# First pair of the second FFN as plain block products inside the pool mixer's last steps, with the pool stage in a written order

## The chip, the cores and the metric

The kernel runs on one core of a Trainium2 chip. The core has a matrix engine (TensorE, PE in the profile), a vector engine (VectorE, DVE), a scalar engine (ScalarE, ACT), a general engine (GpSimd, POOL) and an engine whose queue starts transfers (SyncE, SP); 16 DMA engines move data between HBM and the on-chip memory. Each engine works through its own instructions in their order and waits where an operand is not ready. Times are microseconds (us) of the device for one launch.

## The reference, cut to what matters

Two layers of an encoder over 512 prompt rows and 32 sample rows (544 tokens), model width 1024. Layer 0 mixes with attention and a recurrence, layer 1 with a trailing-window pooling; each mixer is followed by a SwiGLU feed-forward (FFN) of inner width 2816. All is float32.

```
def rmsnorm(x, g):   y = x * rsqrt(mean(x*x) + EPS) * g
def swiglu(x, wg, wu, wd):   return (silu(x @ wg) * (x @ wu)) @ wd

def pool_mixer(xn, buf, start_pos, pool_w, pool_scale):
    for gi, win in enumerate((2, 4, 8, 16)):          # four groups of 256 channels
        outs.append((end - begin) / cnt - xf[:, POOL_BUF:, sl])   # trailing mean minus identity
    y = einsum('btgc,gcd->btgd', stack(outs), pool_w) * pool_scale

for layer in range(2):
    x = x + mixer(rmsnorm(x, norm_mix[layer]))
    x = x + swiglu(rmsnorm(x, norm_ffn[layer]), ffn_gate[layer], ffn_up[layer], ffn_down[layer])
return rmsnorm(x, norm_final), ...states
```

## The kernel before

Activations are held channel-major: `x` is 8 blocks of 128 channels by 544 tokens, and the tokens are cut into two halves of 272. To keep float32 accuracy a product is three matmuls: each operand is split in a high part (rounded by ACT, `AF.Copy` into a reduced type) and a low part (the difference, by DVE); high*high, high*low and low*high are summed in PSUM. "Splitting" a 128x1024 weight tile is one ACT and one DVE instruction (L822, L823).

**FFN.** The 2816 inner channels are 22 blocks f, taken as 11 pairs fp. For a pair, gate and up (u = 0, 1) times the two halves of the 8 channel blocks is a 2x2 block product. It is done with seven products in place of eight (Strassen-Winograd): `strassen` makes 14 steps of 12 matmuls of 272 columns (168 in all), whose weight operands are sums such as t1, t2, t3, t4 and whose activation operands are sums that the class `Forms` builds (b11, n1, n2, b21, t3, t4, b22), once per FFN. `Forms.add(k)` is called for each channel block k as it becomes final; blocks 4 to 7 build all the mixed sums.

`Supply` holds the weights: 17 slots of 128x1024, and a list of operations (load, add, split) with due times counted in beats (`beat.tick`, one per step or per down bank). Sums of weight blocks are formed partly by a second DMA that accumulates (issued by POOL, L836) and partly by DVE (L845). `need(n)` runs the list until n is there. `rows` supplies the down weights; the last pair's rows have the due times in L785.

`down(fp)` adds the hidden blocks of earlier pairs into `x`: 8 banks of 12 or 24 matmuls per pair, in two PSUM buffers `sm`, each followed by a DVE add into `x` (L1000). They are spread over the 14 steps of the pair by L1040. For the pairs 1 and 2 only two hidden blocks are due, so that a bank there is 6 matmuls. `last_down` does the rest of the first FFN's down product (L1019, L1025) and calls `after0`, which makes the norm and splits for the pool mixer. `final` does that for the second FFN together with the output norm.

**Pool stage** (from L1147 on). For six token tiles t and two channel halves i, `pool_in` multiplies by the pool weights (12 matmuls of 256 columns), `pool_mid` evicts with the row's norm factor `rt` (by ACT or DVE in turn), `pool_out(m)` multiplies by the window bands and adds channel block m into `x` (two DVE instructions, L1210), then calls `n3.add(m)`. From m = 4 on the first steps of the second FFN's pair 0 stand between the `pool_out`s. In this stage only PE's order is written by hand (`manual_schedule(engines={PE})`); the order of DVE, ACT and SP is chosen by the compiler's scheduler. In the FFNs the order of PE, DVE, ACT and SP is as written; POOL's is chosen by the scheduler everywhere.

Of the kernel before, what the change touches and what calls it, by code (L numbers as in the profile page):

```python
# [14 lines left out]
P = 128  # L15
# [16 lines left out]
def kernel(  # L32
# [226 lines left out]
    class Forms(Norm):  # L259
# [35 lines left out]
        def add(self, k):  # L295
            j, g = k % 4, col(self.gcol + k)
            x0, x1 = x[:, k, :HN], x[:, k, HN:]
            if k < 4:
                if j % 2 == 0:
                    self.d[j], self.d[j + 1] = self.tmp(j // 2)  # L300
                d = self.d[j]
                self.put("b11", j, x0, g)
                ve.tensor_tensor(d, x0, x1, op=ALU.subtract)
                self.put("n1", j, d, g)
            else:
                d, g0 = self.d[j], col(self.gcol + j)
# [10 lines left out]
            self.square(k)  # L317

# [454 lines left out]
    class Supply:  # L773
# [94 lines left out]

        def ahead(self):
# [33 lines left out]
    ORDER = (("a11", "b11"), ("t1", "n1"), ("t2", "n2"), ("t3", "t3"), ("a12", "b21"), ("a22", "t4"), ("t4", "b22"))  # L903

    def strassen(sup, nin, fp, hid):
# [3 lines left out]
        def product(i, u):  # L909
# [43 lines left out]
            elif i == 5:  # L953
# [5 lines left out]
                hidden(2, out[:, 1], 1)  # L959
# [3 lines left out]
            elif i == 6:  # L963
                ve.tensor_tensor(out[:, 0, h1], o, pb, op=ALU.add)
                beat.later(1, lambda: ve.tensor_mul(out[:, 0], out[:, 0], s[:, 0]))  # L965
                hidden(1, out[:, 0], 0)

        def hidden(n, t, i):
            f = 2 * fp + i
            a, b = [hp.tile([P, T], F32R, tag=f"h{p}{f % 6}", name=nm("h" + p)) for p in "hl"]  # L970

            def low():
                ve.tensor_tensor(b, t, a.bitcast(F32), op=ALU.subtract)
                hid[f] = a, b

            beat.later(n, lambda: ac.activation(a, t, AF.Copy))  # L976
            beat.later(n + 1, low)
# [3 lines left out]
    def ffn(sup, nin, after=None, mid={}, last=None, first=None):  # L981
# [85 lines left out]
    def bands():  # L1067
        eye = big.tile([P, P], F32, name="eye")[:, :BW]
        gp.memset(eye, 1.0)
        band(eye, 1, 15)  # L1070
        eyl = cst.tile([P, NL], F32, name="eyl")[: NL + 15]
        gp.memset(eyl, 1.0)
        band(eyl, 1, 15)
        for g, win in enumerate(WINDOWS):
# [71 lines left out]
    with tc.manual_schedule(engines=queues):  # L1146
        ffn(supply, n1[0], after0, {(0, 3): lambda: scales(n1[0]), (0, 7): lambda: n1[0].out(), (1, 4): bands,  # L1147
# [44 lines left out]
    n3 = Forms(16 + 8, 0)  # L1192

    def pool_out(m):
# [16 lines left out]
        n3.add(m)  # L1211

    with tc.manual_schedule(engines={mybir.EngineType.PE}):
        ps = [(small(), 0), (small("z"), 0), (small("z"), 0)]
        for t in range(3):
            pool_in(ps[t][0], t, 0)
            if t == 2:
                rt = n2.rs_tok([(0, j, a2[:, c : c + n]) for j, (c, n) in enumerate(TS)] + [(0, 6, na30)])
        for t in range(3):
            pool_mid(ps[t][0], t, 0, t % 2)  # L1220
        todo = [(3, 0), (4, 0), (5, 0), (0, 1), (1, 1), (2, 1), (3, 1), (4, 1), (5, 1)]
        for j, (t, i) in enumerate(todo):
            if j % 2 == 0:
                pa = one("pa"), one("pb")
            pool_in(pa[j % 2], t, i)
            if j % 2:
                for b, (t, i) in enumerate(todo[j - 1 : j + 1]):
                    pool_mid(pa[b], t, i, b)
            if j == 5:
                supply.need(("t1", 0))  # L1230
                pool_out(0)
            if j == 7:
                pool_out(1)
        pool_mid(pa[0], 5, 1, 0)
# [3 lines left out]
        prods = strassen(supply, n3, 0, first)
        for m in range(4, KD):
            pool_out(m)  # L1240
            if m == 7:
                give(*ptm, *ptb)
            if m in (4, 6):
                pool_state(m == 6)
            prods.pop(0)()
        prods.pop(0)()
        prods.pop(0)()
        scales(n3)
        for f in prods[:2]:
            f()  # L1250
# [104 lines left out]
```

## Time and profile before

| | us |
|---|---|
| runs of the kernel (3) | 1100.87, 1104.32, 1105.19; median 1104.32 |
| profiled execution, its own time | 1103.79 |
| its span, first to last instruction | 1102.0 |
| PE busy | 1044.4 (95%) |
| DVE busy | 768.4 (70%) |
| ACT busy | 491.7 (45%) |

The span is 1.8 us shorter than the execution's own time. PE is the engine that is nearly always busy, so that what counts are the few places where it waits and those where its clock is lower; matmuls overlap, so that the distance of two starts, and not the length of one, is what a matmul costs. In a row of the timeline the bracket is the idle time ahead of it and what ended it.

### The profile page before, as it was taken

How to read it: one execution, taken by the hardware profiler on the slowest of the kernel's cores; microseconds unless marked ns; L12 is line 12 of the kernel's file. 1: busy time of each engine (PE TensorE's matmuls, PEld its weight loads, DVE VectorE, ACT ScalarE, POOL GpSimd, SP SyncE). 2: the span in 40 equal slices, each digit the busy share in tenths (PEclk: the TensorE clock that was granted, in tenths of full speed). 3: DMA queues.
4: the chain of work that ended last, by engine and by line, in shares of the span. 5: the costliest groups of instructions: out<-in, count | busy, mean ns of one | idle time of the engine just before them, and what ended most of it. 6: DMA issues, size and time to landing. Idle time of an engine off the chain costs nothing.

```text
span 1102.0 us, 19760 instructions
## 1 busy us (share of the span) xinstructions
PE 1044.4 (95%) x7971; PEld 1002.9 (91%) x7971; DVE 768.4 (70%) x1236; ACT 491.7 (45%) x825; POOL 210.7 (19%) x331
## 2 busy tenths in 40 slices
PE   8979999999899999999999989599999999999987
PEld 7978888899899999999999878499999999999976
DVE  6776666767777777767776575957777766677643
ACT  7555555544643344332444354644434434334422
POOL 5162225103421101111110211111011111010100
PEclk8989999999999999999999998889999999999999
DMA  8412222414877467756566532256655676656602
GB/s 221 140 50 68 68 58 90 106 52 106 158 158 144 106 120 168 173 135 132 125 127 153 128 88 34 62 116 148 139 116 122 146 172 149 135 122 125 167 33 81
DMA packets 210955, 130.63 MB, mean 119 GB/s; under 512 B 7224, under 2 KB 195872, under 8 KB 210865
## 3 DMA queue, kind: packets, MB, share of 16 engines
q1 hardware_dynamic: 162528, 103.11, 33.2%
q0 software_dynamic: 47696, 25.16, 17.6%
q8 instruction: 62, 1.02, 0.4%
q10 hardware_dynamic: 640, 1.12, 0.3%
q14 instruction: 29, 0.23, 0.1%
HBM read 124.76 MB, written 4.60 MB: 117 GB/s over the span
## 4 chain that ended last, share of the span: by engine, by line
PE 75%; DVE 10%; issue 6%; ACT 5%; DMA 2%; POOL 1%; SPq 0%; ACTq 0%; DVEq 0%; POOLq 0%
PE xy L925 30%; PE sm L997 17%; PE z L925 11%; PE acc L168 10%; ACT ha L822 2%; DVE la L823 2%; DVE sB L474 1%; DMA raw<-in_hyb_w_in_dram 1%; PE ps L1019 1%; PE pa L1173 1%; POOL sA L493 1%; ACT y L1294 1%; DVE y L1300 1%; DMA rt<-in_ffn_up_dram 1%; DVE lt L823 1%
## 5 line engine op out<-in xcount | busy, mean ns | idle before, releaser
L997 PE MATMUL sm<-hh,h 128*128 128x272 f32 x576 | 168.0, 292 | 7.0 <-DVE x L1000 6.2
L836 POOL DMA_DIRECT2D rt<-in_ffn_gate_dram x44 | 57.0, 1295 | 589.4 <-DMA rt<-in_ffn_gate_dram 382.3
L997 PE MATMUL sm<-hl,h 128*128 128x272 f32 x576 | 165.6, 287 | 0.0
L997 PE MATMUL sm<-hh,l 128*128 128x272 f32 x576 | 165.4, 287 | 0.0
L823 DVE TENSOR_TENSOR lt<-rt,ht 128x1024 fp32r<-128x1024 f32 x88 | 107.9, 1226 | 50.7 <-ACT ht L822 50.6
L997 PEld LDWEIGHTS sm<-hh,h 128*128 128x128 f32 x576 | 108.4, 188 | 11.3 <-DVE x L1000 11.3
L98 ACT ACTIVATE s<-s 128x544 f32<-128x544 f32 x44 | 29.0, 659 | 187.1 <-DVE s L934 182.4
L997 PEld LDWEIGHTS sm<-hh,l 128*128 128x128 f32 x576 | 108.4, 188 | 0.0
L997 PEld LDWEIGHTS sm<-hl,h 128*128 128x128 f32 x576 | 108.4, 188 | 0.0
L925 PE MATMUL xy<-b,ha 128*128 128x272 f32 x704 | 103.6, 289 | 0.8 <-DVE x L678 0.8
L823 DVE TENSOR_TENSOR la<-ra,ha 128x1024 fp32r<-128x1024 f32 x66 | 81.0, 1227 | 29.1 <-ACT ha L822 29.1
L822 ACT ACTIVATE ht<-rt 128x1024 fp32r<-128x1024 f32 x88 | 92.5, 1051 | 11.5 <-DVE rt L845 6.1
L925 PEld LDWEIGHTS xy<-b,ha 128*128 128x128 f32 x704 | 93.9, 188 | 1.3 <-DVE x L678 1.0
L1000 DVE TENSOR_TENSOR x<-x,sm 128x272 f32<-128x272 f32 x160 | 69.2, 432 | 31.8 <-PE sm L997 30.8
L168 PE MATMUL acc<-xh,whi 128*128 128x272 f32 x320 | 75.4, 317 | 2.5 <-ACT xh L98 2.5
L836 POOL DMA_DIRECT2D rt<-in_ffn_up_dram x44 | 76.5, 1739 | 2.0 <-DMA rt<-in_ffn_up_dram 1.5
L976 ACT ACTIVATE hh<-u 128x544 fp32r<-128x544 f32 x44 | 29.0, 659 | 97.5 <-DVE u L965 49.9
L822 ACT ACTIVATE ha<-ra 128x1024 fp32r<-128x1024 f32 x66 | 67.3, 1051 | 6.1 <-DMA ra<-in_ffn_up_dram 4.9
L168 PE MATMUL acc<-xl,whi 128*128 128x272 f32 x320 | 68.2, 294 | 0.5 <-DVE xl L228 0.5
L168 PE MATMUL acc<-xh,wlo 128*128 128x272 f32 x320 | 67.9, 293 | 0.0
L925 PE MATMUL xy<-n,ht 128*128 128x272 f32 x352 | 54.1, 295 | 11.4 <-DVE n L293 6.9
L943 ACT ACTIVATE c<-xy 128x272 f32<-128x272 f32 x44 | 17.5, 398 | 95.2 <-PE xy L925 95.2
(381 smaller groups left out, 2525.1 us busy)
## 6 DMA issues: line engine op xcount, KB each, us to landing
r<-in_ffn_down_dram SPq DMA_DIRECT2D x44, 512.0 KB, 6.0
ra<-in_ffn_gate_dram SPq DMA_DIRECT2D x66, 256.0 KB, 5.3
ra<-in_ffn_up_dram SPq DMA_DIRECT2D x66, 256.0 KB, 6.8
rt<-in_ffn_gate_dram SPq DMA_DIRECT2D x44, 256.0 KB, 3.3
rt<-in_ffn_up_dram SPq DMA_DIRECT2D x44, 256.0 KB, 4.5
rt<-in_ffn_gate_dram POOLq DMA_DIRECT2D x44, 256.0 KB, 6.0
rt<-in_ffn_up_dram POOLq DMA_DIRECT2D x44, 256.0 KB, 7.1
raw<-in_hyb_w_in_dram SPq DMA_DIRECT2D x20, 512.0 KB, 3.9
```

What stands on the lines that cost most here:

```text
L98: i = ac.activation(*a, **k).ins
L168: pe.matmul(ps[:, h, : s.stop - s.start], lhsT=a[:, wi, :], rhs=b[:, s], start=first and j == 0, stop=last and j == 2)
L474: ve.tensor_tensor_scan(r, r, r, 1.0, op0=ALU.mult, op1=ALU.min)
L493: gp.affine_select(t[:, N - P :], t[:, N - P :], pattern=[[-1, P]], compare_op=ALU.is_gt, fill=fill, base=0, channel_multiplier=1)
L822: ac.activation(hi, raw, AF.Copy)
L823: ve.tensor_tensor(lo, raw, hi.bitcast(F32), op=ALU.subtract)
L836: gp.dma_start(v(t)[:, u], w, accum_op=ALU.add)
L925: pe.matmul(o, lhsT=lt, rhs=r, start=first and n == 0, stop=n == 11, skip_group_check=True)
L943: ac.activation(pc, o, AF.Copy)
L976: beat.later(n, lambda: ac.activation(a, t, AF.Copy))
L997: pe.matmul(ps, lhsT=lt[:, c], rhs=r[:, s], start=i == 0 and j == 0, stop=i == len(fs) - 1 and j == 2)
L1000: ve.tensor_add(xs, xs, ps)
```

## The change

1. The second FFN's pair 0 is no longer done by `strassen` but by `plain`: 2 blocks f x 2 (gate, up) x 8 channel blocks x 2 token halves x 3 = 192 matmuls. Its weights are the four plain blocks a11, a12, a21, a22 (8 loads by SP, 4 splits), without t1, t2, t3, t4 (14 loads, 4 of them accumulating by POOL, 7 splits and 2 DVE adds).
2. `LateForms.add(k)` makes only the split of block k's two token halves; DVE's part of block k is held back until the next `pool_out`. The mixed sums for pair 1 come from `sums()`, 16 steps that are placed between the matmuls of the plain pair.
3. The pool stage has its order written for PE, DVE, ACT and SP. All six `pool_in` of the first channel half now stand ahead of the matmuls for the norm (`rs_tok`).
4. For pairs 1 and 2 of both FFNs the down banks come one per step from step 4 on, in place of three in a row behind step 5 and then one per step.
5. The last pair's down rows are due 4 to 10 beats earlier. The window bands are emitted at four places in place of one.

```
-            self.rows(PAIRS, ((-9, -5), (-8, -3), (-3, 3), (-1, 5)))
+            self.rows(PAIRS, ((-15, -9), (-14, -8), (-12, -6), (-11, -4)))
...
+        def plain(self, fp):
+            for j, (t0, t1) in enumerate(((-20, -12), (-18, -10), (-6, 2), (-2, 5))):
+                n = f"a{j // 2 + 1}{j % 2 + 1}", fp
+                self.blocks(t0, n, (2 * fp + j // 2, j % 2))
+                self.split(t1, n, n)
...
-                    for _ in range(0 if n < 5 else 3 if n == 5 else 1):
+                    few = len(sup.due(fp)[0]) < 4
+                    for _ in range(n > 3 if few else 0 if n < 5 else 3 if n == 5 else 1):
...
+    class LateForms(Forms):
+        def add(self, k):
+            g = col(self.gcol + k)
+            bs = [(x[:, k, s], *self.block(k, h)) for h, s in HALVES]
+            for src, h, _ in bs:
+                ac.activation(h, src, AF.Copy, scale=g)
+            t = self.acc if k == 0 else s2.tile([P, T + NS], F32, tag="nsq", name=nm("nsq"), bufs=1)[:, :T]
+            ac.activation(t, x[:, k], AF.Square)
+            def low():
+                for src, h, l in bs:
+                    ve.scalar_tensor_tensor(l, src, g, h.bitcast(F32), op0=ALU.mult, op1=ALU.subtract)
+                if k:
+                    ve.tensor_add(self.acc, self.acc, t)
+            return low
...
+        def mm(i, us, k, bank=None):
+            for u in us:
+                n = f"a{i + 1}{k // 4 + 1}", 0
+                wh, wl = [v(w)[:, u, k % 4] for w in sup.need(n)]
+                for h in range(2):
+                    if k == 0:
+                        acc[i, u, h] = bank()[:, :HN]
+                    bh, bl = nin.block(k, h)
+                    for j, (a, b) in enumerate(((wh, bh), (wh, bl), (wl, bh))):
+                        pe.matmul(acc[i, u, h], lhsT=a, rhs=b, start=k == 0 and j == 0, stop=k == KD - 1 and j == 2,
+                                  skip_group_check=True)
...
+        for t in range(6):
+            into(t, 0)
+        rt = n2.rs_tok([(0, j, a2[:, c : c + n]) for j, (c, n) in enumerate(TS)] + [(0, 6, na30)])
+        into(0, 1)
+        mid(*[(t, 0) for t in range(6)])
...
+        supply.need(("a12", 0))
         pool_out(3)
+        for m in range(4, KD + 4):
+            if m < KD:
+                pool_out(m)
...
+            elif low:
+                low.pop()()
+                sums = n3.sums()
+            beat.tick(supply)
+            mm(0, (0, 1), m - 4, lambda: one("f0"))
...
+        for k in range(KD):
+            mm(1, (0,), k, lambda: small("z"))
+            sums.pop(0)()
+            if k == 2:
+                scales(n3)
         n3.out()
+        for k in range(KD):
+            if k == 1:
+                gate_out(0)
+            if k == 4:
+                up_out(0)
+            mm(1, (1,), k, small)
+            if sums:
+                sums.pop(0)()
+        gate_out(1)
+        beat.later(3, lambda: up_out(1))
```

DVE in the first FFN's `last_down`, before: `x<-x,ps` adds a finished bank, `xs` and `nacc` are the pool mixer's split and norm sum; `la`, `lt` are splits and `rt` a sum of weights for the second FFN's pair 0.

```order
L1025 TENSOR_TENSOR x<-x,ps_7480 128x272
L1025 TENSOR_TENSOR x<-x,ps_7481 128x272
L823 TENSOR_TENSOR la_1119_7874<-ra_1105_7723,ha_1118_7873 128x1024
L823 TENSOR_TENSOR lt_1121_7878<-rt_1104_7718,ht_1120_7877 128x1024
L845 TENSOR_TENSOR rt_1165_8053<-rt_1104_7718,ra_1105_7723 128x1024
L228 SCALAR_TENSOR_TENSOR xs_7536<-x,cols,xs_7536 128x544
L219 TENSOR_TENSOR nacc_7494<-nacc_7494,nsq_7539 128x544
L1025 TENSOR_TENSOR x<-x,ps_7522 128x272
```

The same place in the changed kernel:

```order
L1143 TENSOR_TENSOR x<-x,ps_7480 128x272
L1143 TENSOR_TENSOR x<-x,ps_7481 128x272
L228 SCALAR_TENSOR_TENSOR xs_7536<-x,cols,xs_7536 128x544
L219 TENSOR_TENSOR nacc_7494<-nacc_7494,nsq_7539 128x544
L1143 TENSOR_TENSOR x<-x,ps_7522 128x272
```

The three weight instructions of 128x1024 have left the chain of adds.

PE in pair 1 of the second FFN, before: the first down banks (`sm`), the first two of three in a row, between step 5 (`xy_8470`) and step 6.

```order
L925 MATMUL xy_8470<-n_1147_8014,lt_1230_8448 128x272 x4
L997 MATMUL sm_8560<-hh_8398,h_1237_8486 128x272
L997 MATMUL sm_8560<-hl_8399,h_1237_8486 128x272
L997 MATMUL sm_8560<-hh_8398,l_1238_8487 128x272
L997 MATMUL sm_8560<-hh_8433,h_1237_8486 128x272
L997 MATMUL sm_8560<-hl_8434,h_1237_8486 128x272
L997 MATMUL sm_8560<-hh_8433,l_1238_8487 128x272
L997 MATMUL sm_8570<-hh_8398,h_1237_8486 128x272
L997 MATMUL sm_8570<-hl_8399,h_1237_8486 128x272
```

In the changed kernel the first bank stands behind step 4, and a step of the pair follows it:

```order
L1054 MATMUL xy_8417<-n_1190_8260,lt_1214_8421 128x272 x4
L1115 MATMUL sm_8522<-hh_8461,h_1223_8463 128x272
L1115 MATMUL sm_8522<-hl_8462,h_1223_8463 128x272
L1115 MATMUL sm_8522<-hh_8461,l_1224_8464 128x272
L1115 MATMUL sm_8522<-hh_8378,h_1223_8463 128x272
L1115 MATMUL sm_8522<-hl_8379,h_1223_8463 128x272
L1115 MATMUL sm_8522<-hh_8378,l_1224_8464 128x272
L1054 MATMUL xy_8443<-n_1190_8260,ht_1213_8420 128x272
```

Each bank is now apart from the next by a step of 12 matmuls, and the first one reads the second hidden block (`hh_8461`, `hl_8462`) one step earlier.

DVE behind the last norm sum of the pool stage, in the changed kernel: splits of weights (a22 of pair 0, a11 and t1 of pair 1), then the first of the 16 steps of `sums()`.

```order
L346 TENSOR_TENSOR nacc_7718<-nacc_7718,nsq_8137 128x544
L903 TENSOR_TENSOR la_1180_8173<-ra_1154_8029,ha_1179_8172 128x1024
L903 TENSOR_TENSOR la_1182_8177<-ra_1155_8032,ha_1181_8176 128x1024
L903 TENSOR_TENSOR lt_1184_8205<-rt_1153_8024,ht_1183_8204 128x1024
L378 TENSOR_TENSOR tmp_8154<-x 128x544
L378 TENSOR_TENSOR tmp_8155<-x 128x544
L925 TENSOR_TENSOR rt_1187_8232<-rt_1153_8024,ra_1155_8032 128x1024
L370 SCALAR_TENSOR_TENSOR n_1186_8222<-tmp_8154,cols,n_1185_8221 128x272 x2
L370 SCALAR_TENSOR_TENSOR n_1186_8222<-tmp_8155,cols,n_1185_8221 128x272 x2
L373 SCALAR_TENSOR_TENSOR tmp_8158<-tmp_8154,cols,tmp_8156 128x272 x2
L195 RECIPROCAL rt_8271<-rt_8271 128x4
```

Before, weight splits and the forms for pair 0 alternate here, and pair 0's own steps wait for them:

```order
L823 TENSOR_TENSOR lt_1199_8235<-rt_1166_8055,ht_1198_8234 128x1024
L293 SCALAR_TENSOR_TENSOR t_1154_8029<-tmp_8010,t_1153_8028 128x272
L823 TENSOR_TENSOR lt_1201_8252<-rt_1167_8060,ht_1200_8251 128x1024
L293 SCALAR_TENSOR_TENSOR n_1148_8015<-tmp_8098,n_1147_8014 128x272
L290 TENSOR_TENSOR b_1155_8032<-tmp_8144,b_1155_8032 128x272
L293 SCALAR_TENSOR_TENSOR t_1152_8024<-tmp_8099,t_1151_8023 128x272
```

What the plain pair's matmuls need is made ahead of this place; what is made here is for pair 1.

## Rows read from the trace of the kernel before

**Rows 1.** Busy time by engine in two stretches (span, PE, PEld, DVE, ACT, POOL, clock, DMA).

```profile
700.00:720.00 20.00, 9.33 (x44) 8.27 (x44) 17.42 (x31) 9.23 (x20) 2.69 (x2) 0.66 0.33 71
...
1000.00:1050.00 50.00, 49.89 (x397) 49.46 (x396) 35.37 (x53) 19.52 (x28) 5.73 (x5) 1.00 0.54 128
```

**Rows 2.** Timeline of PE, third bank of a burst (start, length, line, operation, [idle]).

```profile
308.77 0.39 PE L997 MATMUL sm<-hh,h 128*128 128x272 f32 x1 [1.54 <-DVE x L1000]
...
337.68 0.39 PE L997 MATMUL sm<-hh,h 128*128 128x272 f32 x1 [1.54 <-DVE x L1000]
...
747.00 0.39 PE L997 MATMUL sm<-hh,h 128*128 128x272 f32 x1 [1.61 <-DVE x L1000]
...
775.91 0.39 PE L997 MATMUL sm<-hh,h 128*128 128x272 f32 x1 [1.56 <-DVE x L1000]
```

**Rows 3.** Timeline of PE, last down product of the first FFN.

```profile
639.83 0.36 PE L1019 MATMUL ps<-hh,h 128*128 128x272 f32 x1 [0.78 <-DVE x L1025]
...
645.17 0.39 PE L1019 MATMUL ps<-hh,h 128*128 128x272 f32 x1 [2.10 <-DVE x L1025]
```

**Rows 4.** Timeline of DVE at that place.

```profile
639.95 1.22 DVE L823 TENSOR_TENSOR la<-ra,ha 128x1024 fp32r<-128x1024 f32 x1
641.09 1.22 DVE L823 TENSOR_TENSOR lt<-rt,ht 128x1024 fp32r<-128x1024 f32 x1
642.22 1.22 DVE L845 TENSOR_TENSOR rt<-rt,ra 128x1024 f32<-128x1024 f32 x1
```

**Rows 5.** Timeline of PE at the start of the output stage.

```profile
1065.69 0.41 PE L1285 MATMUL sm<-h,hh 128*32 128x512 f32 x1 [2.69 <-ACT h L822]
...
1066.95 0.42 PE L1285 MATMUL sm<-l,hh 128*32 128x512 f32 x1 [0.61 <-DVE l L823]
```

**Rows 6.** Timeline of PE in the pool stage.

```profile
663.19 2.33 PE L243 MATMUL sm<-ones,nacc 128*128 128x1 f32 x12 [4.48 <-DVE nacc L219]
...
671.35 0.40 PE L1173 MATMUL pb<-pwh,xs 128*128 128x256 f32 x2
...
672.78 0.40 PE L1173 MATMUL pa<-pwh,xs 128*128 128x256 f32 x2
...
675.63 0.38 PE L1207 MATMUL z<-bf,ptm 128*128 128x128 f32 x2
...
677.17 0.51 PE L1173 MATMUL pa<-pwh,xs 128*128 128x256 f32 x2
```

**Rows 7.** Timeline of PE, norm sums in the first FFN.

```profile
272.12 1.10 PE L243 MATMUL sm<-ones,nacc 128*128 128x1 f32 x10
```

**Rows 8.** Timeline of PE, pair 0 and pair 1 of the second FFN.

```profile
700.34 1.27 PE L925 MATMUL z<-n,ht 128*128 128x272 f32 x8 [1.98 <-DVE x L1210]
...
711.81 0.59 PE L925 MATMUL xy<-n,ht 128*128 128x272 f32 x1 [3.44 <-ACT n L292]
714.53 0.59 PE L925 MATMUL xy<-n,ht 128*128 128x272 f32 x1 [2.12 <-DVE n L293]
...
734.70 1.17 PE L925 MATMUL xy<-b,ha 128*128 128x272 f32 x8
...
736.21 1.17 PE L925 MATMUL xy<-b,ha 128*128 128x272 f32 x8
...
743.74 0.28 PE L997 MATMUL sm<-hh,h 128*128 128x272 f32 x1
```

**Rows 9.** Timeline of DVE in the pool stage.

```profile
693.04 0.49 DVE L1210 SCALAR_TENSOR_TENSOR x<-sm,cols,x 128x272 f32<-128x272 f32 x1
693.46 0.71 DVE L219 TENSOR_TENSOR nacc<-nacc,nsq 128x544 f32<-128x544 f32 x1
694.09 0.43 DVE L293 SCALAR_TENSOR_TENSOR n<-tmp,n 128x272 fp32r<-128x272 f32 x1
```

**Rows 10.** Timeline of ACT at the second FFN's norm factor.

```profile
720.90 1.28 ACT L92 ACT_TABLE_LOAD   x1
```

More of the change, by code (lines that the diff above doesn't have):

```diff
@@ L773, with __init__ @@
     class Supply:
-        def __init__(self, l):
+        def __init__(self, l, plain=False):
             self.l, self.raw, self.w, self.start = l, {}, {}, None
@@ L781, in __init__ @@
             for fp in range(PAIRS):
-                self.base = 22 * fp - 8 * bool(fp)
-                self.pair(fp)
+                self.base = 22 * fp - (6 if plain else 8) * bool(fp)
+                (self.pair if fp or not plain else self.plain)(fp)
             self.base += 22
-            self.rows(PAIRS, ((-9, -5), (-8, -3), (-3, 3), (-1, 5)))
+            self.rows(PAIRS, ((-15, -9), (-14, -8), (-12, -6), (-11, -4)))
             self.ops.sort(key=lambda o: o[0])
@@ L903, with hidden, low, plain @@
     ORDER = (("a11", "b11"), ("t1", "n1"), ("t2", "n2"), ("t3", "t3"), ("a12", "b21"), ("a22", "t4"), ("t4", "b22"))
+    def hidden(n, t, f, hid):
+        a, b = [hp.tile([P, T], F32R, tag=f"h{p}{f % 6}", name=nm("h" + p)) for p in "hl"]
+        def low():
+            ve.tensor_tensor(b, t, a.bitcast(F32), op=ALU.subtract)
+            hid[f] = a, b
+        beat.later(n, lambda: ac.activation(a, t, AF.Copy))
+        beat.later(n + 1, low)
+    def plain(sup, nin, hid):
+        s, out = [sc.tile([P, 2 * T], F32, tag=t, bufs=1, name=nm(t)).rearrange("p (f c) -> p f c", f=2) for t in "su"]
+        acc = {}
+        def mm(i, us, k, bank=None):
[9 more added lines that the diff above has]
+                                  skip_group_check=True)
+            if k % 4 == 3 and us[-1]:
+                sup.done(n)
+        def gate_out(i):
+            for h, c in HALVES:
+                ve.tensor_mul(s[:, i, c], acc[i, 0, h], nin.r[:, c])
+            beat.later(1, lambda: act(s[:, i], s[:, i], AF.Silu))
+            beat.later(2, lambda: ve.tensor_mul(s[:, i], s[:, i], nin.r))
+        def up_out(i):
+            for h, c in HALVES:
+                ve.tensor_mul(out[:, i, c], acc[i, 1, h], s[:, i, c])
+            hidden(1, out[:, i], i, hid)
+        return mm, gate_out, up_out
     def strassen(sup, nin, fp, hid):
@@ L958, in product @@
                 beat.later(1, up)
-                hidden(2, out[:, 1], 1)
+                hidden(2, out[:, 1], 2 * fp + 1, hid)
             elif i == 6 and u == 0:
@@ L965, in product @@
                 beat.later(1, lambda: ve.tensor_mul(out[:, 0], out[:, 0], s[:, 0]))
[L966 to L977, printed above, removed]
+                hidden(1, out[:, 0], 2 * fp, hid)
         return [lambda i=i, u=u: product(i, u) for i in range(7) for u in range(2)]
@@ L1065, in band, with bands @@
         gp.affine_select(o, o, pattern=[[-1, n]], compare_op=ALU.is_ge, fill=0.0, base=win - 1 - off, channel_multiplier=1)
[L1067 to L1074, printed above, removed]
+    eye = big.tile([P, P], F32, name="eye")[:, :BW]
+    eyl = cst.tile([P, NL], F32, name="eyl")[: NL + 15]
+    def bands(*gs):
+        if 0 in gs:
+            gp.memset(eye, 1.0)
+            band(eye, 1, 15)
+            gp.memset(eyl, 1.0)
+            band(eyl, 1, 15)
+        for g in gs:
+            win = WINDOWS[g]
             gp.memset(bf[:, g], 1.0 / win)
@@ L1190, in pool_state @@
         gp.dma_start(pl_p[0, 0][:, 512 * hf : 512 * (hf + 1)], so[15:30])
-    n3 = Forms(16 + 8, 0)
+    n3 = LateForms(16 + 8, 0)
+    low = []
     def pool_out(m):
@@ L1210, in pool_out @@
             ve.scalar_tensor_tensor(xs, pp[:, :HN], col(40 + m), xs, op0=ALU.mult, op1=ALU.add)
[L1211 to L1234, printed above, removed]
+        if low:
+            low.pop()()
@@ new lines, in pool_out, with into, mid @@
+        low.append(n3.add(m))
+    with tc.manual_schedule(engines=queues):
+        supply = Supply(1, plain=True)
+        for _ in range(2):
+            supply.ops.pop(0)[2]()
+        banks = {}
+        def into(t, i):
+            banks[t, i] = (small if t == 0 and not i else lambda: small("z") if t < 3 and not i else one("pi"))()
+            pool_in(banks[t, i], t, i)
+        def mid(*ts):
+            for n, (t, i) in enumerate(ts):
+                pool_mid(banks[t, i], t, i, n % 2)
+        for t in range(6):
[3 more added lines that the diff above has]
+        mid(*[(t, 0) for t in range(6)])
+        into(1, 1)
+        into(2, 1)
+        mid((0, 1), (1, 1))
+        pool_out(0)
+        into(3, 1)
+        mid((2, 1))
+        into(4, 1)
+        pool_out(1)
+        mid((3, 1))
+        into(5, 1)
@@ L1235 @@
         pool_out(2)
+        mid((4, 1), (5, 1))
+        supply.need(("a12", 0))
         pool_out(3)
         first = {}
[L1238 to L1250, printed above, removed]
-        n3.out()
@@ L1252 @@
-        for f in prods[2:]:
-            f()
+        mm, gate_out, up_out = plain(supply, n3, first)
+        for m in range(4, KD + 4):
+            if m < KD:
+                pool_out(m)
+                if m in (4, 6):
+                    pool_state(m == 6)
+                if m == 7:
+                    give(*ptm, *ptb)
+            elif low:
+                low.pop()()
+                sums = n3.sums()
+            beat.tick(supply)
+            mm(0, (0, 1), m - 4, lambda: one("f0"))
+            if m == KD + 3:
+                sums.pop(0)()
+                sums.pop(0)()
```

62 lines of the change are left out of this document (58 added, 4 removed).

## Prediction

> **What bounds the kernel now.** I read first the busy times by slice and the clock, then the chain of waits, then the brackets in PE's timeline, and last DVE's and ACT's timelines at the places where PE waits. The first view shows that PE has no room over most of the span: in a stretch of the second FFN it is busy for 49.9 of 50 us at full clock, with DVE at 35.4 [rows 1]. There a saving on another engine is worth nothing, and a matmul more costs its distance: twelve of 272 columns take 736.21 - 734.70 = 1.51 us, 0.126 each [rows 8]. The second view puts nearly all of the rest on DVE and ACT. The brackets tell where. Up to a few long ones in the first half that the change doesn't touch, they are four kinds:
> - behind two banks of a down burst, PE waits for DVE's add into `x`: 1.54, 1.54, 1.61, 1.56 [rows 2], in pairs 1 and 2 of each FFN, sum 6.25;
> - in the first FFN's last down product, 0.78 and 2.10 [rows 3], sum 2.88;
> - at the start of the output stage, 2.69 and 0.61 [rows 5], sum 3.30;
> - in the pool stage and the second FFN's pair 0: 4.48 ahead of the norm sums [rows 6], then five gaps of 2.0 to 3.4 between 698 and 715 [rows 8]. Here PE has 9.3 us of work in 20, DVE 17.4, and the clock is 0.66 [rows 1]: DVE is the engine that sets the pace.
>
> **The change part by part.** All is reckoned in the profiled execution, 1103.79 us (its span of 1102.0 and 1.8 around it), 0.5 under the median of the runs.
>
> *Bursts.* Three banks of six matmuls (0.75 us each) stand in a row, with two buffers; the third needs the first one's add, which stands on DVE behind a weight split. With one bank per step, 1.51 us of other matmuls come between two banks. All four brackets go: -6.25. What is late next: the first bank now comes one step earlier and reads the hidden blocks of the pair before; in three of the four cases those are split by ordinary steps with a step's time in hand. The fourth, behind the plain pair, is in the stage's sum below. If the cover is missing, each place keeps about what it had.
>
> *Last down product.* Between two adds DVE does two splits and a sum of weights for the old pair 0: 639.95 to 643.36, three at a distance of 1.14 [rows 4]; PE waits behind them. They move behind the pool stage's start, where they are counted below: -2.88.
>
> *Down rows of the last pair.* Four splits of 1.14 (4.6 on DVE) go into the last pair's steps, where DVE has 14.6 us of 50 free [rows 1]; the output stage's two brackets go, since nothing else is late there (the hidden blocks are made by the last pair's own steps): -3.30. If that cover were gone, the price would be at most the 3.30.
>
> *Bands.* They are emitted later, but POOL's own order stays as it was but for four accumulating loads that are gone: 0. POOL has 5.7 us of 50 busy in the FFN [rows 1]; were a band's work to fall ahead of an accumulating load, the load still has a dozen beats until its split.
>
> *Pool stage and pair 0.* I take it from the end of the third `pool_in` (663.19 - 4.48 = 658.7) [rows 6] to the first down bank of pair 1, 743.74 [rows 8]: 85.0 us before. For the new order I walk the three written queues, each instruction starting when its engine is free and its operands are there.
>
> PE alone: nine `pool_in` at 1.43 (672.78 - 671.35), eight `pool_out` at 1.54 (677.17 - 675.63) [rows 6], the plain pair's 192 matmuls at 0.126 (24.2; 24 more than before, 3.0), five steps of pair 1 (7.6), two sets of norm sums at full clock (about 1.4 and 1.1, by 1.10 for ten [rows 7]), some 1.5 for small transposes: 12.9 + 12.3 + 24.2 + 7.6 + 2.5 + 1.5 = 61.0. It would be there at 719.7. The three `pool_in` that now stand ahead of the norm sums fill the 4.48; one wait for a PSUM buffer of about 1.4 comes in its place, since the evictions need the norm. `pool_out(3)` ends at about 680.6.
>
> DVE from there to the split of the second hidden block, which the first bank reads: five `pool_out` updates and six low splits (22 of 272), mixed sums (16 of 272), the gates and products of the plain pair (8), so 46 at 0.42; 18 of 544 at 0.63 [rows 9]; nine of 1024 (splits of a11, a12, a21, a22, of a11, t1 and t2 of pair 1, one of down rows, and one sum) at 1.14 [rows 4]: 19.3 + 11.3 + 10.3 = 40.9, with small things 41.5, so 722 if it never waits. In the walk it waits 9.4 more: twice for ACT's half of a weight split that stands behind squares (1.7 and 2.4), 2.4 at the root of the norm, where ACT reloads its table (1.28 [rows 10]) on both sides of it, and the rest in pieces under 1.2. So the second hidden block is split at 732, and the bank starts at 732.2. PE's waits in the walk: about 2.0 ahead of `pool_out(4)`, 3.5 ahead of the norm's spread, 2.1 at step 2 of pair 1 (its `z` bank is held until DVE has read the plain pair's gate), 1.7 at the bank.
>
> Before, six steps precede the first bank, now five: one step, 1.51, is still to come. 732.2 + 1.5 = 733.7, against 743.74: -10.0. DVE saves three splits and two sums (5.7) and has half of its forms' work behind the plain matmuls; PE pays 3.0. Bounds: PE's order alone gives 719.7 + 1.5, so -22.5; DVE without a wait gives 722.5 + 1.5, so -19.7; with twice the waits 741.6 + 1.5, so -0.6. I take the walk's own value, as its durations are rows of the same instructions.
>
> Sum: -6.25 - 2.88 - 3.30 - 10.0 = -22.4; 1103.8 - 22.4 = **1081.4 us**.
>
> The clock: after the 4.48 without matmuls the norm sums are at half rate, 2.33 for twelve against 1.10 for ten [rows 6, 7], the lower of the two levels, 1.2 GHz in place of 2.4; after 1.98 the next eight matmuls take 1.27 against 1.17, so full [rows 8]. The gap of 3.5 lies between. The Trainium skill (TensorE: Matmul & The Clock Gate, "HAM oscillation — how this bites in real kernels") says that waits between bursts drop the array to half rate, so that each next burst starts slow; the rows agree for the long gap and not for the short one. By that rule the second half of the plain pair would run at half rate, 48 matmuls and 6.0 us longer; by the row of 1.98, none. As DVE is behind PE there by 3.8 (2.1 and 1.7), the sum by the rule would be 1081.4 + 2.2.
>
> **The rivals.**
> - *PE sets the pace* (DVE and ACT never late). For: 41.5 us of DVE against 39 of PE from `pool_out(3)` on. Against: the root of the norm sits in ACT's queue behind the second step of `sums()`. Time: 1081.4 - 9.7 (DVE's bound) = 1071.7, by PE's bound 1068.9.
> - *The stage gains nothing.* The order written by hand has waits in series that the walk sees too small (ACT, DVE, ACT for each form, PSUM buffers held by late evictions); twice the 9.4 does it. For: each wait is on an engine that stands still with work behind it. Against: five gaps and half rate are to be beaten. Time: 1103.8 - 12.4 + 0 to -0.6 = 1091.
> - *The bursts don't go:* the bank one step earlier waits for the hidden block as long as it did for the add. For: it is 2.3 us sooner. Against: no bracket shows PE waiting for a hidden block now. Time: 1081.4 + 6.25 = 1087.7.
> - *Slower: the clock.* PE falls to half rate at the norm gap or earlier and, with the gaps at `pool_out(4)`, step 2 and the bank, stays there. Each us of matmuls then costs one more, first against DVE's lead. From `pool_out(4)` to the first bank PE has 39 us of work; all of it at half rate ends at 680.6 + 78 = 758.6, so 26.4 later than forecast, 1107.8. It decides from about 35 us of full-rate work done slowly (22.4 and the 12.5 by which DVE is later than PE). For: the stretch from 700 to 720 at 0.66 now [rows 1]. Against: full rate after 1.98.
>
> **How the numbers follow.** Forecast 0.60 (own range 1076 to 1087), PE sets the pace 0.16, stage gains nothing 0.14, bursts stay 0.06, slower by the clock 0.04. The range for 8 in 10 runs from near the first rival's time to the second's: 1071 to 1092. A measurement of this kernel can tell about 0.5% (5.5 us) from no change. All cases but the last lie below 1098.8: faster 0.94; the last one's smaller forms share the rest, within 0.03, slower 0.03.
>
> **What would show it.** In the profile after: no bracket behind L1118 in pairs 1 and 2, none in the first last down product, none behind ACT at the first output matmuls; the norm sums of the pool stage right behind the sixth `pool_in`; `pool_out(3)` done 22 us behind the third `pool_in`; DVE without gaps over 2.5 us from there; the first down bank 73 to 74 us behind the third `pool_in`, with PE's largest gap (3 to 4) ahead of the norm's transposes. It would be wrong if ACT stood idle while DVE waits for a load (t1 of pair 1 late), if the clock were under 0.8 between `pool_out(4)` and pair 1, or if a bracket of over 3 us stood at the first bank.

## The result, and the profile after

The changed kernel takes 1085.19 us (median of 4 runs, 1083.86 to 1085.57) against 1104.51 before (4 runs): a ratio of 0.983, 95% interval 0.981 to 0.985. Forecast were 1081.4 and a range of 1071 to 1092: the direction and the range hold, the gain is 4 us short. The profiled execution, in which the forecast was reckoned, took 1085.57, 18.2 less than that of before. One of the six runs of the kernel with the old due times, below, took 1265.58 at a granted clock of 0.75; what is said of that kernel goes by the other five.

The busy times of the two stretches of [rows 1], from the view by windows (span, PE, PEld, DVE, ACT, POOL, clock, DMA), and the stretch of the plain pair:

```profile
700.00:720.00 20.00, 12.97 (x90) 12.47 (x90) 16.59 (x34) 12.38 (x22) 0.00 (x0) 0.83 0.32 69
1000.00:1050.00 50.00, 49.52 (x381) 46.92 (x380) 34.31 (x55) 18.93 (x26) 3.16 (x3) 1.00 0.43 117
...
677.00:723.00 46.00, 35.33 (x250) 34.14 (x251) 36.97 (x69) 27.16 (x47) 4.81 (x6) 0.85 0.29 70
```

The last row is the one to look at: in these 46 us PE is idle for 10.7 and DVE for 9.0. No engine is full, so waits in series set the pace, and the clock is at 0.85.

Next PE's timeline of after (start, length, line, operation, [idle before it and what ended it]): the four waits of over 2 us that are left from the first FFN's end on, and the places of the old brackets.

```profile
619.48 5.31 PE L1241 MATMUL sm<-pw,hist 128*15 128x256 f32 x16 [2.36 <-DVE hist L1237]
...
657.25 1.30 PE L243 MATMUL sm<-ones,nacc 128*128 128x1 f32 x12
...
680.64 1.01 PE L1305 MATMUL sm<-ident,pst 128*30 128x128 f32 x4 [3.83 <-DVE x L1330]
...
710.11 0.79 PE L203 MATMUL sm<-ident,rt 128*128 128x128 f32 x5 [2.44 <-DVE rt L195]
715.49 0.82 PE L1016 MATMUL sm<-b,ha 128*128 128x272 f32 x2 [4.60 <-ACT rs L204]
...
719.06 0.42 PE L1016 MATMUL sm<-tmp,ha 128*128 128x272 f32 x2
...
730.76 0.29 PE L1115 MATMUL sm<-hh,h 128*128 128x272 f32 x1
...
733.01 0.29 PE L1115 MATMUL sm<-hh,h 128*128 128x272 f32 x1
...
735.26 0.29 PE L1115 MATMUL sm<-hh,h 128*128 128x272 f32 x1
...
1047.73 0.42 PE L1436 MATMUL sm<-h,hl 128*32 128x512 f32 x1 [0.42 <-DVE hl L996]
```

Gone are the four third-bank brackets of [rows 2] (730.76, 733.01 and 735.26 start the first three banks of pair 1, without one), both of [rows 3] and both of [rows 5]; 0.42 is left at the output stage. The norm sums run without a wait at full rate, 1.30 against 2.33 in [rows 6]. New are 3.83 and 4.60, and a 2.36 ahead of the matmuls with the history (`hist`), which stood at 1.39 before (a row of the kernel before that was not among those above):

```profile
623.23 3.63 PE L1119 MATMUL sm<-pw,hist 128*15 128x256 f32 x16 [1.39 <-DVE hist L1115]
```

The same 16 matmuls took 3.63 there and take 5.31 now. The first two matmuls behind the 4.60 take 0.82, two of the same shape at 719.06 0.42: half rate, then full. Cut into stretches by the start of such matmuls, the 18.2 that the span lost stand against the forecast like this (us; a minus is a gain):

| stretch | forecast | measured |
|---|---|---|
| start to pair 0's first product | 0 | -1.2 (267.50 to 266.34; such starts spread over 265.3 to 268.4 in all the kernels, so this is chance) |
| from there to the history matmuls | -3.1 (two bursts) | -2.6 |
| history matmuls to the first last-down matmul | 0 | +1.7 (half rate) |
| last down product, to the third `pool_in` | -2.9 | -3.6 |
| third `pool_in` to pair 1's first bank | -11.5 (85.0 to 73.5) | -7.3 (85.0 to 77.7) |
| first bank to output stage (two bursts, one step later) | -1.7 | -2.3 |
| output stage | -3.3 | -2.9 |

The end of the third `pool_in` is that of its last matmul before, and the start of the next one in the changed kernel, 0.17 ahead of such an end; counted alike, the two rows there are -3.4 and -7.5. The stage is short by 4.2 (4.0 counted alike), and the history matmuls cost 2.7 that were forecast nowhere (0.97 of longer wait, 1.7 of slow matmuls). The rest leans the other way, 1.2 of it by chance.

The norm factor goes round by all three engines: PE sums the squares, ACT takes the root (L98), DVE the reciprocal (L195), PE spreads it over all rows into two `sm` banks (L203), and ACT copies these out (L204, L205). What held PE for 4.60 stands in ACT's timeline of after:

```profile
708.19 1.28 ACT L92 ACT_TABLE_LOAD   x1
709.49 0.40 ACT L98 ACTIVATE rt<-sm,eps 128x4 f32<-128x4 f32 x2
709.90 1.28 ACT L92 ACT_TABLE_LOAD   x1
711.20 0.66 ACT L358 ACTIVATE n<-tmp 128x544 fp32r<-128x544 f32 x1
713.47 0.66 ACT L358 ACTIVATE t<-tmp 128x544 fp32r<-128x544 f32 x1 [1.62 <-DVE tmp L373]
714.30 0.66 ACT L358 ACTIVATE t<-tmp 128x544 fp32r<-128x544 f32 x1 [0.17 <-DVE tmp L373]
714.86 0.58 ACT L204 ACTIVATE rs<-sm 128x512 f32<-128x512 f32 x1
```

PE's spread of the norm is done at 710.9, but L204, which empties its bank, starts at 714.86, behind a table load and three steps of the mixed sums. The plain pair's last 48 matmuls want those same two `sm` banks. The Trainium skill (TensorE: Matmul & The Clock Gate, "Architectural detail: the array is 16× 32×32, not 1× 128×128") calls ACT's and DVE's queues strictly first in, first out; this trace agrees: 4.0 us pass between L204's data and its start. The 3.83 has its cause in DVE's timeline:

```profile
677.32 2.36 DVE L903 TENSOR_TENSOR la<-ra,ha 128x1024 fp32r<-128x1024 f32 x2 [1.59 <-ACT ha L902]
679.60 0.49 DVE L1330 SCALAR_TENSOR_TENSOR x<-z,cols,x 128x272 f32<-128x272 f32 x1
680.01 0.49 DVE L1330 SCALAR_TENSOR_TENSOR x<-sm,cols,x 128x272 f32<-128x272 f32 x1
```

`pool_out(3)` is through PE at 674.5; its update of `x` waits behind two weight splits, which wait for ACT; with it waits the `sm` bank that PE needs at 676.8.

### The profile page after: what moved, and what is told of

Same layout as the page of the kernel before. It is cut to its first block, busy times and chain, and to the rows that moved or that the text cites. A ratio compares the mean times of both kernels' runs of the same rounds, so it can differ in the third digit from the quotient of the medians.

```text
span 1083.9 us, 19767 instructions
## 1 busy us (share of the span) xinstructions
PE 1042.1 (96%) x7995; PEld 1001.6 (92%) x7995; DVE 760.1 (70%) x1222; ACT 488.8 (45%) x814; POOL 205.5 (19%) x327
## 4 chain that ended last, share of the span: by engine, by line
PE 77%; DVE 9%; issue 5%; ACT 4%; DMA 2%; POOL 2%; ACTq 0%; SPq 0%; DVEq 0%; POOLq 0%
PE xy L1054 28%; PE sm L1115 17%; PE z L1054 11%; PE acc L168 10%; PE ps L1137 2%; DVE la L903 2%; ACT ha L902 1%; DVE sB L554 1%; PE pi L1292 1%; DMA rt<-in_ffn_up_dram 1%; DMA sB<-in_x_prompt_dram 1%; PE sm L1016 1%; POOL sA L573 1%; ACT y L1445 1%; DVE y L1451 1%
## 5 line engine op out<-in xcount | busy, mean ns | idle before, releaser
L916 POOL DMA_DIRECT2D rt<-in_ffn_gate_dram x42 | 54.4, 1296 | 574.9 <-DMA rt<-in_ffn_gate_dram 341.5
L903 DVE TENSOR_TENSOR lt<-rt,ht 128x1024 fp32r<-128x1024 f32 x84 | 103.0, 1227 | 46.9 <-ACT ht L902 46.7
L98 ACT ACTIVATE s<-s 128x544 f32<-128x544 f32 x44 | 29.0, 659 | 173.3 <-DVE s L1063 171.0
L1054 PE MATMUL xy<-b,ha 128*128 128x272 f32 x672 | 98.3, 289 | 0.8 <-DVE x L758 0.8
L902 ACT ACTIVATE ht<-rt 128x1024 fp32r<-128x1024 f32 x84 | 88.2, 1050 | 5.5 <-DMA rt<-in_ffn_up_dram 3.2
L1054 PEld LDWEIGHTS xy<-b,ha 128*128 128x128 f32 x672 | 89.6, 188 | 1.0 <-DVE x L758 1.0
L1118 DVE TENSOR_TENSOR x<-x,sm 128x272 f32<-128x272 f32 x160 | 69.2, 433 | 28.9 <-PE sm L1115 27.9
L168 PEld LDWEIGHTS acc<-xh,whi 128*128 128x128 f32 x320 | 50.2, 192 | 9.3 <-issue 5.7
```

What stands on the lines that cost most here:

```text
L98: i = ac.activation(*a, **k).ins
L168: pe.matmul(ps[:, h, : s.stop - s.start], lhsT=a[:, wi, :], rhs=b[:, s], start=first and j == 0, stop=last and j == 2)
L902: ac.activation(hi, raw, AF.Copy)
L903: ve.tensor_tensor(lo, raw, hi.bitcast(F32), op=ALU.subtract)
L916: gp.dma_start(v(t)[:, u], w, accum_op=ALU.add)
L1054: pe.matmul(o, lhsT=lt, rhs=r, start=first and n == 0, stop=n == 11, skip_group_check=True)
```

## The experiments

All were timed against the kernel before on the same chip, in three groups; that kernel's own median was 1103.73, 1102.46 and 1102.89 there and 1104.51 beside the changed kernel. Medians of different groups thus differ by up to 2 us without any change, and only the old bursts, the stage alone, "both", "the root first" and the best one have a 95% interval of the ratio apart from the changed kernel's. What the other five do is told by their traces. "Stage" is the time from the third `pool_in` (as in the table) to pair 1's first down bank in PE's timeline: 77.7 in the changed kernel. The four others that leave its order alone have 77.0 to 78.1 (a step of 1.5 taken off where the bank comes one step later). Theory A says that PE's waits for banks are what the stage lost, rival B that DVE's work sets the pace.

**The stage alone** (old burst rule, old due times, old bands; the lines of the bands are left out).

```
     few = len(sup.due(fp)[0]) < 4
-    for _ in range(n > 3 if few else 0 if n < 5 else 3 if n == 5 else 1):
+    for _ in range(0 if n < 5 else 3 if n == 5 else 1):
...
-    self.rows(PAIRS, ((-15, -9), (-14, -8), (-12, -6), (-11, -4)))
+    self.rows(PAIRS, ((-9, -5), (-8, -3), (-3, 3), (-1, 5)))
```

> The pool stage and the plain pair as changed; the burst rule, the down rows' due times and the bands as before. The trace after has the first down bank of pair 1 77.7 us behind the end of the third pool_in, where 73.5 was forecast and 85.0 stood before with one step more. Theory (the stage's term alone was mis-sized, the terms add up): about -5.8 against before, 1098 us in the profiled execution, the third-bank brackets of pairs 1 and 2 (1.5 to 1.6 each) and those of the first last down product (2.9) back. Rival 1 (the stage's term was right, the other terms too large): -10.0, 1094. Rival 2 (the stage gains only because the down splits went): within 2 of before, 1102 to 1104.

1095.93, a ratio of 0.9926 (0.9904 to 0.9949). Rival 2 falls. The median is 7.8 under the kernel before, with some 5.6 to 10.6 by the interval, which does not tell the theory's 5.8 from rival 1's 10.0. The stage does: 79.6, with one step (1.5) more ahead of the bank, so 5.4 gained, and rival 1 falls. The last down product's brackets did not come back: from its first matmul to the third `pool_in` 28.40, 28.35 with the whole change, 31.93 before. I had put them to the down rows here; the prediction had them right: the old due times do not bring them back, and pair 0's splits are gone from there in this kernel too. Against these gains the profiled run lost 1.5 in the first FFN and 1.0 at the output stage, where half rate followed the 2.69:

```profile
1058.18 0.63 PE L1436 MATMUL sm<-h,hh 128*32 128x512 f32 x1 [2.69 <-ACT h L902]
```

**The old burst rule alone** (the first three lines of that diff).

> The changed kernel with the old burst rule alone (three banks in a row at the end of a short pair). Theory: each of the four places has its bracket of 1.5 to 1.6 back, +6.25 against the changed kernel, 1091.8 us. Rival (DVE behind in pair 1 of the second FFN was the reason there, and it is behind less now): two to three brackets only, +3.1 to +4.7, 1088.7 to 1090.3.

1093.27, ratio 0.9903 (0.9881 to 0.9925): 8.1 over the changed kernel by the medians, 6.6 by the spans of the profiled runs. Four brackets are back, 1.55, 1.54, 1.54 and 1.55, sum 6.18; two of them in PE's timeline:

```profile
738.53 0.39 PE L1115 MATMUL sm<-hh,h 128*128 128x272 f32 x1 [1.54 <-DVE x L1118]
...
767.46 0.39 PE L1115 MATMUL sm<-hh,h 128*128 128x272 f32 x1 [1.55 <-DVE x L1118]
```

The theory holds, and the rival, fewer brackets, falls; what the medians have beyond the brackets is within the 2 us by which groups differ.

**The old due times alone** (the last two lines).

> The changed kernel with the old due times of the last pair's down rows alone. Theory: 2.9 in the first FFN's last down product and 3.3 at the start of the output stage come back, +6.2 against the changed kernel, 1091.8 us. Rival 1: only the first FFN's part, or only the output stage's, +2.9 to +3.3, 1088.5 to 1088.9. Rival 2: the late splits also fall into the pool stage, where DVE is late, and cost there too: above +6.2.

1088.20, ratio 0.9863 (0.9839 to 0.9887): 3.0 over the changed kernel, rival 1. Its PE shows why it is so little:

```profile
617.82 3.62 PE L1241 MATMUL sm<-pw,hist 128*15 128x256 f32 x16 [1.39 <-DVE hist L1237]
...
1046.44 0.64 PE L1436 MATMUL sm<-h,hh 128*32 128x512 f32 x1 [2.70 <-ACT h L902]
```

The output stage has its 2.70 back and runs at half rate behind it (0.64 against 0.41 in [rows 5]): 43.8 from its first matmul to the end, 38.4 in the changed kernel. The history matmuls are 1.39 and 3.62 again: the new due times cost there what they bring elsewhere in part.

**The copies ahead of two steps of the sums.**

```
-            sums.pop(0)()
+            if k < 6:
+                sums.pop(0)()
             if k == 2:
                 scales(n3)
```

> The changed kernel, with the two steps of the mixed sums (t3) that stand ahead of the norm's spread on ACT's queue put behind it; nothing else. Theory A (PE's wait of 4.60 for the two small PSUM banks, which ACT's copies of the spread norm hold, is the shortfall): the copies come right behind the first n step, at about 712 in place of 714.9, the wait falls to 1.5 to 1.9, and the first down bank comes 2.7 to 4.3 earlier (the slow matmuls behind the wait may go too): 1081.3 to 1082.9 us. Rival B (DVE sets the pace: it has split the second hidden block at 729.7, and the bank starts at 730.8): at most 1.1 from this and a new bracket at the first bank, 1084.5 to 1085.6.

1080.95, ratio 0.9801 (0.9775 to 0.9826). ACT, then PE, in this kernel:

```profile
712.12 0.66 ACT L358 ACTIVATE n<-tmp 128x544 fp32r<-128x544 f32 x1
712.69 0.58 ACT L204 ACTIVATE rs<-sm 128x512 f32<-128x512 f32 x1
```

```profile
711.03 0.79 PE L203 MATMUL sm<-ident,rt 128*128 128x128 f32 x5 [2.44 <-DVE rt L195]
713.32 0.82 PE L1016 MATMUL sm<-b,ha 128*128 128x272 f32 x2 [1.50 <-ACT rs L204]
...
728.91 0.39 PE L1115 MATMUL sm<-hl,h 128*128 128x272 f32 x1 [0.25 <-DVE hl L996]
```

The wait falls from 4.60 to 1.50 and the stage from 77.7 to 74.3: 3.4 for 3.1 of wait, where rival B has at most 1.1 and the rest lost again at the first bank; the bracket there is 0.25. Theory A: DVE did not set the pace, but it is close behind.

**The norm put earlier.**

```
-            sums.pop(0)()
-            if k == 2:
-                scales(n3)
-        n3.out()
+            if k == 0:
+                scales(n3)
+            sums.pop(0)()
+            if k == 4:
+                n3.out()
```

> The changed kernel, with the third norm's sums, root and spread put some steps earlier into the plain pair's first half (sums at its first step, spread at the fifth), so that neither the root nor the copies stand behind the mixed sums on ACT. Theory A (PE's waits at the spread and at the two banks, 2.44 and 4.60, and 1.5 of slow matmuls behind, are what the stage lost): both waits go, the first down bank comes up to 8.5 earlier, 1077 us. Rival B (DVE sets the pace): DVE loses only its own waits there (2.30, 0.37, 0.58) and the 1.1 by which it was ahead of the bank, 3.5 to 4.5 earlier, 1081 to 1082, and PE's brackets come back at pair 1's steps or at its first bank.

1082.12, ratio 0.9815 (0.9797 to 0.9832), stage 74.0: 3.7 gained, B's number and not A's 8.5. The wait for the banks is gone, but PE now waits 3.05 ahead of the spread, and 0.34 and 0.69 at the first bank:

```profile
707.09 0.97 PE L203 MATMUL sm<-ident,rt 128*128 128x128 f32 x5 [3.05 <-DVE rt L195]
...
726.80 0.39 PE L1115 MATMUL sm<-hl,h 128*128 128x272 f32 x1 [0.69 <-DVE hl L996]
```

B's reason isn't thereby shown: the root may still stand too far back on ACT. "The root first" below answers it.

**The two splits put earlier.**

```
         mid((0, 1), (1, 1))
+        supply.need(("a12", 0))
         pool_out(0)
...
-        supply.need(("a12", 0))
         pool_out(3)
```

> The changed kernel, with the two weight splits of the plain pair (a11, a12) emitted ahead of pool_out(0) instead of ahead of pool_out(3), where DVE waits 1.59 for ACT's half, works 2.28 on them, and PE waits 3.83 for the update of x behind them. Theory: DVE and ACT have idle time of 2 to 4 us at 661 to 666, the splits fit there, and all that follows on both engines comes about 3.8 earlier: 1081.8 us (PE's slow matmuls from 681 to 685 may become full ones; DVE decides). Rival 1: pool_out(0) and what hangs on it come later by as much, 1085 to 1086. Rival 2: the gain is taken up by the later waits (the norm's root, the two banks), which end at the same time: 1084 to 1085.6.

1081.35, ratio 0.9805 (0.9788 to 0.9821), stage 72.8: 4.9 gained, more than the 3.8. DVE's timeline, and PE at the transposes:

```profile
663.61 2.35 DVE L903 TENSOR_TENSOR la<-ra,ha 128x1024 fp32r<-128x1024 f32 x2
665.88 0.50 DVE L1330 SCALAR_TENSOR_TENSOR x<-z,cols,x 128x272 f32<-128x272 f32 x1
...
675.96 0.48 DVE L1330 SCALAR_TENSOR_TENSOR x<-z,cols,x 128x272 f32<-128x272 f32 x1
```

```profile
677.04 0.61 PE L1305 MATMUL sm<-ident,pst 128*30 128x128 f32 x4
```

The splits fill idle time (rival 1 falls), DVE comes to the update of `x` without a gap, the transposes start without a bracket and take 0.61 in place of 1.01. The 4.59 ahead of the last half stays, and rival 2 falls: a wait ahead of another was real time.

**Both.** The two diffs above together.

> The norm put earlier and the two splits put earlier, together. If DVE sets the pace after pool_out(3) and each of the two takes away its own waits: the gains add, 7 to 8.5 less than the changed kernel, 1077 to 1078.5. If PE's waits were the loss: 12, 1073. If the two take away the same slack: no more than the larger of the two alone, 1081 to 1082.

1077.46, ratio 0.9766 (0.9749 to 0.9783), stage 68.9: 8.8 gained, where 3.7 and 4.9 make 8.6, so the gains add. What is left shows on DVE and PE:

```profile
703.89 0.29 DVE L195 RECIPROCAL rt<-rt 128x4 f32<-128x4 f32 x2 [3.28 <-ACT rt L98]
```

```profile
704.21 1.33 PE L203 MATMUL sm<-ident,rt 128*128 128x128 f32 x5 [3.07 <-DVE rt L195]
```

The root stands on ACT behind eight steps of the sums (698.87 to 702.28) and a table load.

**The root first.** As "both", with the two calls at new places again:

```
             if m == KD + 3:
+                scales(n3)
                 sums.pop(0)()
...
+            if k == 2:
+                n3.out()
```

> The two splits early as before, and the third norm's sums and root put ahead of the first step of the mixed sums (before, in the kernel with both put early, they stood behind eight ACT steps of it: DVE waited 3.28 for the root and PE 3.07 for the spread); the spread at the third step of the half. The changed kernel has 1085.2, that kernel 1077.5. If the queue order on ACT was the cause of those two waits: DVE's 3.28 becomes under 0.5, PE's 3.07 under 1, and the first down bank comes 68.9 - 3 = 65 to 66 us behind the third pool_in, 1073.5 to 1075; then DVE sets the pace, and the rest of PE's lead (some 3) shows as brackets at pair 1's steps or first bank. If DVE's work alone set the pace already: 68 to 69, 1077.

1075.40, ratio 0.9743 (0.9721 to 0.9766), 0.4 above the range that was expected; its interval overlaps that of "both", so the trace decides. Stage 65.8, 3.1 less, as expected of the order on ACT. DVE's 3.28 and PE's 3.07 are gone. The brackets of over 0.5 that PE has left from there to the output stage:

```profile
704.97 0.52 PE L1016 MATMUL sm<-b,ha 128*128 128x272 f32 x2 [0.99 <-ACT rs L204]
714.78 1.27 PE L1054 MATMUL z<-n,ht 128*128 128x272 f32 x8 [0.52 <-DVE s L1023]
720.24 0.39 PE L1115 MATMUL sm<-hh,h 128*128 128x272 f32 x1 [0.68 <-ACT hh L999]
721.32 0.40 PE L1115 MATMUL sm<-hl,h 128*128 128x272 f32 x1 [0.69 <-DVE hl L996]
```

So it was the order on ACT here too, not DVE's work. Now the second hidden block is late: the two waits that the prediction had seen (step 2's `z` bank and the first bank) show together only here, at 0.5 and 1.4 in place of 2.1 and 1.7.

**The best one.** As the last, with the old due times in the first FFN (`plain` is true for the second FFN alone).

```
-            self.rows(PAIRS, ((-15, -9), (-14, -8), (-12, -6), (-11, -4)))
+            self.rows(PAIRS, ((-15, -9), (-14, -8), (-12, -6), (-11, -4)) if plain else ((-9, -5), (-8, -3), (-3, 3), (-1, 5)))
```

> The same with the old due times of the down rows in the first FFN (the new ones stay in the second, where they take 3 off the output stage). The matmuls with the history behind the first FFN's last product start 2.36 behind PE's last work and, in most runs, at half rate (5.24 to the first down matmul); with the old due times 1.39 and 3.55. Theory (the earlier splits keep DVE late there): 0.97 less where the clock stays full, 2.66 where it falls: 1 to 2.7 less than the kernel without this edit. Rival (the 2.36 comes from the burst rule or the bands): 0.

1072.81 (1070.79 to 1075.03), ratio 0.972 (0.9695 to 0.9745): 12.4 under the changed kernel, and its interval lies apart from that one's: faster than it and than the kernel before. That it is also faster than the last one, by 2.6, the overlapping intervals do not show; the rows do. The history matmuls come behind 1.39 and take 3.63. Its stage in the view by windows:

```profile
675.00:717.00 42.00, 39.37 (x305) 37.73 (x304) 36.74 (x69) 28.58 (x49) 7.38 (x8) 1.00 0.49 104
```

PE is busy for 39.4 of 42 at full clock, where the changed kernel had 35.3 of 46 at 0.85.

**Those due times alone** in the changed kernel.

> The changed kernel with the old due times of the down rows in the first FFN alone; nothing else. Theory: the wait ahead of the history matmuls 1.39 in place of 2.36 and full rate behind it, the output stage as after, so 2.66 less: 1082.5. Rival 1 (the wait comes from the burst rule): 2.36 again and 1085. Rival 2 (the first FFN's last down product gets brackets back): 1085 to 1088.

1082.93, ratio 0.9815 (0.9793 to 0.9838): 2.3 less by the medians, which the intervals do not tell from no change. PE's timeline does:

```profile
618.19 3.63 PE L1241 MATMUL sm<-pw,hist 128*15 128x256 f32 x16 [1.39 <-DVE hist L1237]
```

The wait is 1.39 again, the matmuls take 3.63, and neither the last down product (28.39) nor the output stage (38.3) loses. Both rivals fall. Why DVE's copy of the history comes 0.97 later with the new due times stands in its timeline, the last split of a down row (`l<-r,h`) in the changed kernel and then in this one:

```profile
613.50 1.23 DVE L903 TENSOR_TENSOR l<-r,h 128x1024 fp32r<-128x1024 f32 x1 [1.67 <-ACT h L902]
```

```profile
613.21 1.22 DVE L903 TENSOR_TENSOR l<-r,h 128x1024 fp32r<-128x1024 f32 x1
```

Two such splits stand in the 11 us ahead of the copy in both kernels (with the old due times two more come behind it). With the new due times the second one stands ahead of an add into `x` and a gate product (L1118, L1065) and DVE waits 1.67 for ACT's half of it; with the old ones it stands behind them and waits for nothing. All seven kernels with a wait of 2.34 to 2.36 on PE have that 1.67 or 1.68 on DVE, and none of the five with 1.39 has it.

## Why the prediction was right and where not

- *Bursts*: right, 6.25 forecast, 6.18 by the run that puts them back. The first bank, one step earlier, waited nowhere in pairs 1 and 2 of the changed kernel. (In "the root first" and with those due times alone, a bank of the first FFN's pair 1 waits 0.72 and 0.73 for a down row's split.)
- *Last down product*: right in cause (the run of the stage alone), 3.6 measured for 2.9 (3.4 counted alike).
- *Down rows*: the output stage gave 2.9 for 3.3. The step that failed is "go into the last pair's steps, where DVE has 14.6 us of 50 free": true on average, but in the first FFN one split came ahead of its half from ACT, so that DVE stood for 1.67 and was 0.97 late at the very end of the pair, where PE waits for its copy of `hist`. That cost 0.97, and 1.7 more where the clock fell.
- *Bands*: put at 0; not tried alone.
- *Pool stage*: the mechanism held up to `pool_out(3)` (21.5 behind the third `pool_in`, forecast 21.9), and DVE's three long waits were sized well: 1.59 and 2.24 behind ACT's split halves (1.7 and 2.4), 2.30 at the root (2.4). Its whole way from there to the split of the second hidden block took 55.1, 42.6 of work and 12.5 of waits, where 41.5 and 9.4 were forecast: 1.72 and 0.79 of these waits are for PE, which came late itself. What failed is the list of PE's waits in the walk: it has nothing between the spread and the plain pair's last 48 matmuls, where 4.60 stood, since the banks' release was not followed through ACT's queue; and about 2.0 at `pool_out(4)` where 3.83 stood behind it. (The waits that it names, 1.4, 2.0, 3.5, 2.1 and 1.7, make 10.7, and its bank at 73.5 needs 12.5 over PE's 61.0: 1.8 of its own sum stood nowhere.) The 1.4 for a PSUM buffer was 0.69 and the 3.5 ahead of the spread 2.44, which was not PE's largest gap. With DVE later through PE, the forecast waits at step 2 and at the first bank (3.8) did not appear: PE itself came late. The bank stood at 77.7 and not 73.5. With the three orders mended it stands at 65.8.
- *Clock*: the forecast put the fall at the one long wait; it fell at each of 2.36, 3.83 (0.50 from 680 to 684) and 4.60 in the changed kernel, and 677 to 723 ran at 0.85. The rule of the Trainium skill (TensorE: Matmul & The Clock Gate, "HAM oscillation — how this bites in real kernels"), that waits between bursts make the next burst start slow, agrees with these rows (the last section has others that it does not fit). The price that the prediction had for it, 6.0 for the last 48 matmuls, was too high: they took 7.7 (715.49 to 723.23) in place of 6.05, so 1.7; full rate came back during them.
- *Rivals*: PE did not set the pace in the changed kernel; the stage gained; the bursts went; full rate came back each time, so slower by the clock did not come about.

## What to carry to other kernels

In these traces a PSUM bank came free only when the engine that empties it got there in its queue (L204 4.0 us behind its data), so a wait for a bank is mended in the evictor's order. Three changes of order on ACT and DVE (the norm, the splits, the root) took 3.1 to 4.9 us each off the stage, with the same work. Where a stage has no full engine, look at what stands in each queue between data and its reader; a walk must carry every buffer's release through it. And a slack of 15 us in 50 did not cover a split that stood in DVE's queue ahead of its half from ACT: what a queue waits for counts, not only what it works.

## What was not expected of the hardware

The granted clock is not settled by the length of a wait alone. The 16 history matmuls come behind the same wait of 2.34 to 2.36 in seven of the kernels; in five they take 5.31, in two (the norm put earlier, and both) 3.63:

```profile
619.78 3.63 PE L1241 MATMUL sm<-pw,hist 128*15 128x256 f32 x16 [2.36 <-DVE hist L1237]
```

Behind 1.39 (five kernels) they always take 3.62 or 3.63. So too at the output stage: behind 2.69 full rate before [rows 5], behind 2.69 half rate in the stage alone, behind 2.70 half rate with the old due times. And around a wait of 2.11 or 2.12 in the first FFN's pair 0 the granted clock falls in ten kernels and not in two; the changed kernel and "the root first":

```profile
280.00:290.00 10.00, 9.35 (x59) 8.73 (x60) 9.56 (x12) 6.02 (x11) 6.77 (x6) 0.83 0.25 71
```

```profile
280.00:290.00 10.00, 7.83 (x58) 7.39 (x59) 9.15 (x9) 7.21 (x12) 6.54 (x10) 1.00 0.30 54
```

What tells the cases apart no row here shows. Whether it changes from one execution of a kernel to the next was not tried. It makes 1.7 us at the first place and up to 2.5 at the second (43.8 to the end with the old due times, 42.3 in the stage alone, 41.3 before), and the walk had no term for it.
